# A block of Fourier mixing and latent attention: other queues and engines at the start, queries first, the last rows written directly

## The chip, the cores and the metric

The kernel runs on one core of a Trainium2 chip. The metric is the device time of one execution in microseconds (us); lower is better. The engines are named as in the profile: PE is TensorE's matmul, PEld its weight load, DVE is VectorE, ACT is ScalarE, POOL is GpSimd, and SP is SyncE, which here only issues transfers.

## The reference

One layer of a diffusion backbone: 1024 latent tokens and 256 context tokens, 1024 channels, float32. Cut to what matters:

```python
mod = jax.nn.silu(c) @ w_ada[l] + b_ada[l]
sh_m, sc_m, gt_m, sh_f, sc_f, gt_f = jnp.split(mod[:, None, :], 6, axis=-1)
h_lat = modulate(rms_norm(x, g_pre_mix[l]), sh_m, sc_m)      # h * (1 + scale) + shift
p_lat = h_lat @ w_in[l]
u_f, q_a, kv_a, kr_raw = jnp.split(p_lat, [512, 768, 896], axis=-1)
...
kn_l, v_l = mla_keys_values(kv_a, g_kv_a[l], w_kv_b[l])
qn_l, qr_l = mla_queries(q_a, g_q_a[l], w_q_b[l])            # 8 heads, 64 + 32 channels
attn_l = mla_attention(qn_l, qr_l, k_nope, k_rope, v_all)    # latent and context keys
four_l = fourier_mix(u_f, w_fourier[l])                      # real part of a 2-D DFT, then a map
y_lat = jnp.concatenate([four_l, attn_l], axis=-1) @ w_out[l]
x = x + gt_m * rms_norm(y_lat, g_post_mix[l])
h2 = modulate(rms_norm(x, g_pre_ffn[l]), sh_f, sc_f)
x = x + gt_f * rms_norm(swiglu(h2, w_gate[l], w_up[l], w_down[l]), g_post_ffn[l])
```

## The kernel before, in words

Every matrix product is made of three matmuls: each operand is split into a high part, rounded to PE's fast format, and a low part, the rest (`split`, `mm3`). A letter says which engine makes each part: "a" is ACT, "v" is DVE, "p" is POOL. `mm3` issues high by high (L68), low by high (L69) and high by low (L70).

The scheduler of the language orders the instructions of each engine by the order of the code and their dependences; `pin` keeps some of them in the order of the program. Transfers on SP's queue are issued in their order.

**The sweep (`first_tiles`, 0 to 68 us).** Token tiles 0 and 1 (`xs`, 128x1024 each) are loaded, scaled by their `rstd` and transposed (`xT`). Then eight steps `j`, one for each 128 channels. A step loads a piece of w_ada_mix (`araw`, two transfers of 512 KB) and one of w_in (`wraw`, 128x928), splits both (`ah`, `al`; `win` high and low), multiplies the conditioning vectors by the first (16 matmuls to `aps`), turns the result through `arow` into columns (`cps`), makes shift and scale (`SH`, `A`), modulates (`h`), splits that (`hh`, `hl`) and adds 12 matmuls to `acc`. `modulation` runs two steps ahead of `acc`, the loads three. `constants` loads `rows`, from which the conditioning vectors and biases come.

**The Fourier stage (`fourier`, about 153 to 210 us).** `positions(g)` is the DFT over positions of channel group g (24 matmuls to `po`, `pm`, `pp`; the result `z` is split). `last_turn` transposes the last context tile (`rps`). `attention_weights` loads and splits the weights of queries (`wq`, two pieces `wqraw`), keys (`wk`) and values (`wv`), and the transposed queries, keys and values (`qT`, `kvT`); `kr32T` is the rotary part of the keys, split to `K0h`, `K0l`. Then come `keys([0])` (`kps`, split to `K0h`, `K0l`) and `queries(0)` (`qps`, rotated to `q`, split to `Qh`, `Ql`), and the maps of the Fourier weights (`mps`, split to `map0`, `map1`, from `wfpair` and `ch`). Behind them `channels(g)` (`Sp`, `Co`, `Ce`) is interleaved with the score maxima of head 0 (`greatest`: `sps` on PE, `mx` on DVE).

**The end (`down`).** Eight row tiles i of the output. The last group of products for a half of the columns goes over rows 0 to 7 in the passes n = 2, 5, and for the other half in n = 3, 4. In the last passes each row is added up (V, L1190), its squares are summed on ACT, `rstd` comes from POOL (L1212), DVE multiplies by `rstd` and the gate `Gf` (L1170), and POOL adds the row to `out` by an accumulating DMA (L1171). Only row 7 is multiplied by `Gf` beforehand (L1205, L1209), added to x1, which was loaded back from `out`, and written in two plain halves (L1175, L1176). `finish` handles the row before; it stands ahead of the `rstd` of the present one.

Of the kernel before, what the change touches and what calls it, by code (L numbers as in the profile page):

```python
# [18 lines left out]
P = 128  # L19
D = 1024  # L20
# [19 lines left out]
class Block:  # L40
# [126 lines left out]
    def constants(self):  # L167
        tc, nc, t, cst = self.tc, self.nc, self.t, self.cst
        rows = cst.tile([P, P], F32, name="rows")
        nc.sync.dma_start(rows[0:NROWS, :], t["rows"])  # L170
        self.ident = cst.tile([P, P], F32, name="ident")
        nc.sync.dma_start(self.ident, t["ident"])
        self.comb = cst.tile([4, 2], F32, name="comb")
        self.mhalf = cst.tile([P, 2], F32, name="mhalf")
        nc.vector.memset(self.mhalf, -0.5)
        self.ones = cst.tile([P, P], F32, name="ones")
        nc.vector.memset(self.ones, 1.0)
        nc.scalar.activation(rows[0:16, :], rows[0:16, :], AF.Silu)
# [12 lines left out]
        self.A = cst.tile([P, 2, KT], F32, name="A")  # L191
        self.SH = cst.tile([P, 2, KT], F32, name="SH")
        self.A2 = cst.tile([P, KT], F32, name="A2")
        self.SH2 = cst.tile([P, KT], F32, name="SH2")
        self.Gm = cst.tile([P, D], F32, name="Gm")


    def normed(self, src):
# [3 lines left out]
        nc.sync.dma_start(xs, src)  # L202
# [15 lines left out]
    def first_tiles(self):  # L218
# [8 lines left out]
        def win_split(j):  # L227
# [3 lines left out]
            self.split(wh, wl, raw, "a", "p")  # L231
            return wh, wl
        xT = sw.tile([P, KT, 2 * P], F32, name="xT")
        xs = [self.normed(t["x"][i * P:(i + 1) * P, :]) for i in range(2)]
# [14 lines left out]
        def modulation(j, ah, al):  # L249
# [6 lines left out]
            nc.vector.tensor_copy(row, ps[0:4, 0:256])  # L256
# [7 lines left out]
            nc.vector.tensor_scalar(h, xT[:, j, :], self.A[:, 0, j:j + 1], self.SH[:, 0, j:j + 1], ALU.mult, ALU.add)  # L264
# [210 lines left out]
    def fourier(self):  # L475
# [48 lines left out]
        self.split(wfh, wfl, wf, "a", "p")  # L524
        self.split(chh, chl, ch, "a", "p")
        run(positions(0))
        self.last_turn(bank)
        run(weights)
        run(positions(1))
        run(self.keys([0], bank))  # L530
        run(self.queries(0, bank, self.early, self.early, fp, "raw", "S"))
# [7 lines left out]
        for g in range(4):  # L539
            for work in [channels(g)] + ([positions(g + 2)] if g < 2 else []):  # L540
                for _ in work:

                    steps += 1
                    if steps <= len(KCH) * NT:
                        next(filler)
        run(filler)


    def attention_weights(self):
# [8 lines left out]
        raws = [self.fp.tile([P, D], F32, name="wqraw", tag="X", bufs=2) for _ in range(2)]  # L558
        rawk, rawv = (self.fp.tile([P, 512], F32, name="wkraw", tag="S", bufs=2) for _ in range(2))
        nc.sync.dma_start(rawk, t["w_k"])  # L560
        for k in range(2):
            nc.sync.dma_start(raws[k], t["w_q"][k * P:(k + 1) * P, :])
        nc.sync.dma_start(self.ropeq[64:128, :], t["ropeq"])
        nc.sync.dma_start(rawv, t["w_v"])
        def weight(w, raw, g):

            nc.scalar.activation(w[0], raw, AF.Copy, scale=self.cols[:, g:g + 1])
            nc.vector.scalar_tensor_tensor(w[1], raw, self.cols[:, g:g + 1], w[0].bitcast(F32), ALU.mult, ALU.subtract)
        weight(self.wk, rawk, R_GKV)
        for k in range(2):  # L570
            w = [w[:, k, :] for w in self.wq]
            if k:
                weight(w, raws[k], R_GQ + k)
            else:
                nc.gpsimd.tensor_scalar(raws[k], raws[k], self.cols[:, R_GQ + k:R_GQ + k + 1], 0.0, ALU.mult, ALU.add)
                self.split(*w, raws[k], "a", "p")
            self.split(*(x[:, k, :] for x in self.qT), self.q32[:, k, :], "a", "v")
        yield
        self.split(*self.kvT, self.kv32, "a", "v")
        self.split(kh[64:96, :], kl[64:96, :], self.kr32[64:96, :], "a", "p")  # L580
# [93 lines left out]
    def keys(self, heads, bank):  # L674
        m = 64 * len(heads)
        c = slice(64 * heads[0], 64 * heads[0] + m)
        for c0, n in KCH:
# [3 lines left out]
            for i, h in enumerate(heads):  # L681
                kh, kl = self.K[h % 3]
                self.split(kh[0:64, cs], kl[0:64, cs], ps[i * 64:(i + 1) * 64, 0:n])
# [219 lines left out]
    def all_loads(self):  # L903
# [9 lines left out]
        i = NT - 1  # L913
        yield self.raw(("x1", i), t["out"][i * P:(i + 1) * P, :])
# [195 lines left out]
    def down(self):  # L1110
# [50 lines left out]
        rows = [x[:, q].rearrange("p h c -> p (h c)") for x in (up, low) for q in range(4)]  # L1161
        pending = []

        def finish():

            while pending:
                i, r = pending.pop()
                where = t["out"][i * P:(i + 1) * P, :]
                if i + 1 < NT:
# [4 lines left out]
                for cs in (slice(0, 512), slice(512, D)):  # L1174
# [3 lines left out]
        for n, zh, wh in (2, 0, 0), (5, 1, 1), (3, 0, 1), (4, 1, 0):  # L1178
# [5 lines left out]
            for qs in ([0, 1], [2, 3]) if first else ([0], [1], [2], [3]):  # L1184
# [6 lines left out]
                for q in qs:  # L1191
# [3 lines left out]
                    final = i + 1 == NT  # L1195
                    v = f1.tile([P, 1], F32, name="var", bufs=16)
                    if first:
# [6 lines left out]
                        if final:  # L1204
                            pin(V(c, c, self.Gf[:, cs], ALU.mult))  # L1205
                    else:
                        finish()
                        if final:
                            pin(V(c, c, self.Gf[:, cs], ALU.mult))  # L1209
                        nc.scalar.activation(v, s, AF.Identity, bias=ss[i])  # L1210
                        r = f1.tile([P, 1], F32, name="rstd", bufs=4)
                        pin(nc.gpsimd.tensor_tensor(r, v, self.mhalf[:, 0:1], ALU.pow))  # L1212
                        pending.append((i, r))
# [67 lines left out]
```

## Time and profile before

| what | us |
|---|---|
| median of three runs | 1302.64 (1301.27 to 1303.33) |
| profiled execution, its own time | 1300.21 |
| its span | 1298.4 |
| PE busy | 1222.3 (94%) |
| DVE busy | 934.2 (72%) |
| ACT busy | 633.5 (49%) |
| POOL busy | 479.4 (37%) |
| mean granted clock of PE | 0.982 of full speed |

The span runs from the first instruction to the last event of one profiled execution. Busy times are sums over an engine's instructions; an engine that is not busy waits for another, for a transfer or for its queue. In a timeline a row has the start, the duration, the engine, the line, the operation, and `out<-in` by the program's names; in brackets stands how long the engine had been idle and who ended that.

### The profile page before, as it was taken

Reading aid. Unit: us, or ns where it says so; the run is one execution under the profiler, and the core shown is the slowest. Engines: PE = TensorE matmul, PEld = TensorE weight load, DVE = VectorE, ACT = ScalarE, POOL = GpSimd, SP = SyncE. Lnnn points to the kernel's source line nnn. Section 1 sums busy time; section 2 is a strip of 40 time slices with the busy share of each in tenths; the row PEclk is TensorE's granted clock in tenths of the full one; section 3 lists DMA queues with packets and bytes.
Section 4 is the critical chain, followed back from the end, with each engine's and each line's share of the span. In section 5 each row is a group of like instructions: output and inputs, shape, how many; then the busy total and the mean of one; then the engine's idle time right before and its main releaser. Section 6 shows DMA issues by size and latency. Waiting matters only on the chain.

```text
span 1298.4 us, 15437 instructions
## 1 busy us (share of the span) xinstructions
PE 1222.3 (94%) x5474; PEld 955.1 (74%) x5474; DVE 934.2 (72%) x1301; ACT 633.5 (49%) x1045; POOL 479.4 (37%) x333
## 2 busy tenths in 40 slices
PE   5899978979999999889999999999999999999995
PEld 4588866756666666668788888888888887888884
DVE  6866586687675765353689887777777875898795
ACT  5467747646757668255644444433444433221232
POOL 4365556434555453253263332333311300000173
PEclk9999989989999999999999999999999999999998
DMA  8375211011110104642125554434454468987537
GB/s 318 127 246 169 69 49 36 31 33 46 38 33 17 34 18 139 179 140 101 60 81 179 178 178 149 150 110 144 163 178 154 153 212 335 344 296 256 194 130 130
DMA packets 79369, 181.64 MB, mean 140 GB/s; under 512 B 9569, under 2 KB 41332, under 8 KB 79292
## 3 DMA queue, kind: packets, MB, share of 16 engines
q1 hardware_dynamic: 67228, 137.89, 31.8%
q10 hardware_dynamic: 10800, 39.06, 7.7%
q0 software_dynamic: 1264, 3.70, 1.8%
q8 instruction: 43, 0.70, 0.2%
q14 instruction: 34, 0.28, 0.1%
HBM read 129.15 MB, written 51.48 MB: 139 GB/s over the span
## 4 chain that ended last, share of the span: by engine, by line
PE 49%; issue 2%; ACT 2%; POOL 2%; DVE 1%; DMA 1%; POOLq 0%; DVEq 0%; SPq 0%; ACTq 0%
PE gu L69 10%; PE gu L70 10%; PE gu L68 10%; PE y L774 5%; PE dn L68 4%; PE dn L70 4%; PE dn L69 4%; DMA unit<-zu 1%; DMA raw<-w_down 1%; POOL T L58 0%; POOL out_dram L1171 0%; PE T L209 0%; ACT H L321 0%; POOL rstd L1212 0%; DVE rows L1170 0%
## 5 line engine op out<-in xcount | busy, mean ns | idle before, releaser
L50 ACT ACTIVATE unit<-raw 128x512 fp32r<-128x512 f32 x171 | 105.5, 629 | 226.2 <-PE gu L70 106.3
L58 POOL TENSOR_TENSOR pl<-p,ph 128x1024 fp32r<-128x1024 f32 x53 | 128.8, 2431 | 148.0 <-ACT ph L50 111.6
L56 DVE TENSOR_TENSOR unit<-raw,unit 128x512 fp32r<-128x512 f32 x171 | 149.3, 881 | 27.3 <-ACT unit L50 26.9
L715 DVE TENSOR_REDUCE mx<-sps 128x1 f32<-128x512 f32 (+1 forms) x192 | 105.5, 594 | 31.5 <-PE sps L714 30.6
L640 ACT ACTIVATE p<-S 128x1024 f32<-128x1024 f32 x80 | 81.7, 1022 | 87.1 <-PE S L637 76.6
L935 POOL TENSOR_TENSOR s<-raw 128x512 f32<-128x512 f32 x22 | 33.8, 1537 | 241.4 <-DMA raw<-w_gate 167.9
L1155 POOL TENSOR_TENSOR rows<-rows,acc 128x512 f32<-128x512 f32 x8 | 13.5, 1705 | 212.8 <-DVE acc L1138 211.5
L50 ACT ACTIVATE ph<-p 128x1024 fp32r<-128x1024 f32 x80 | 84.3, 1057 | 1.9
L69 PE MATMUL gu<-T,unit 128*128 128x512 f32 x176 | 69.4, 394 | 0.9 <-POOL T L58 0.9
L70 PE MATMUL gu<-Bh,unit 128*128 128x512 f32 x176 | 69.4, 394 | 0.5 <-DVE unit L56 0.5
L68 PE MATMUL gu<-Bh,unit 128*128 128x512 f32 x176 | 69.4, 394 | 0.0
L69 PE MATMUL gu<-Bl,unit 128*128 128x512 f32 x176 | 69.3, 394 | 0.0
L70 PE MATMUL gu<-T,unit 128*128 128x512 f32 x176 | 69.3, 393 | 0.0
L68 PE MATMUL gu<-T,unit 128*128 128x512 f32 x176 | 69.2, 393 | 0.0
L68 PE MATMUL dn<-unit 128*128 128x512 f32 x148 | 58.2, 393 | 0.4 <-ACT unit L50 0.4
L70 PE MATMUL dn<-unit 128*128 128x512 f32 x148 | 58.0, 392 | 0.0
L69 PE MATMUL dn<-unit 128*128 128x512 f32 x148 | 58.0, 392 | 0.0
L621 PE MATMUL O<-pl,Vh 128*65 128x512 f32 x160 | 53.3, 403 | 4.6 <-POOL pl L58 3.8
L345 PE MATMUL acc<-win,hh 128*128 128x512 f32 (+1 forms) x224 | 55.8, 368 | 0.9 <-ACT hh L50 0.6
L1083 DVE TENSOR_TENSOR u<-u,gu 128x512 f32<-128x512 f32 x66 | 44.8, 681 | 15.6 <-PE gu L70 15.0
L78 POOL TENSOR_TENSOR rstd<-var,mhalf 128x1 f32<-128x1 f32 x44 | 27.6, 629 | 76.3 <-DVE var L76 75.6
L774 PE MATMUL y<-woh,xth 128*128 128x512 f32 x128 | 52.5, 410 | 2.4 <-ACT xth L50 2.4
(425 smaller groups left out, 3552.9 us busy)
## 6 DMA issues: line engine op xcount, KB each, us to landing
zu<-zpair ACTq DMA_DIRECT2D x50, 512.0 KB, 4.3
unit<-zu SPq DMA_DIRECT2D x47, 512.0 KB, 4.6
adraw<-w_ada SPq DMA_DIRECT2D x32, 512.0 KB, 3.9
units<-zu SPq DMA_DIRECT2D x27, 512.0 KB, 5.5
zu<-zone ACTq DMA_DIRECT2D x24, 512.0 KB, 3.1
raw<-w_gate SPq DMA_DIRECT2D x22, 512.0 KB, 4.2
raw<-w_up SPq DMA_DIRECT2D x22, 512.0 KB, 6.3
raw<-w_down SPq DMA_DIRECT2D x22, 512.0 KB, 5.2
```

Source lines behind the costliest of these rows:

```text
L50: nc.scalar.activation(hi, src, AF.Copy)
L56: self.lastv = nc.vector.tensor_tensor(lo, src, hi.bitcast(F32), ALU.subtract)
L58: nc.gpsimd.tensor_tensor(lo, src, hi.bitcast(F32), ALU.subtract)
L68: self.nc.tensor.matmul(out, ah, bh, start=i == 0, stop=False)
L69: self.nc.tensor.matmul(out, ah, bl, start=False, stop=False)
L70: self.nc.tensor.matmul(out, al, bh, start=False, stop=i == n - 1)
L345: nc.tensor.matmul(acc[:, o], a[:, k, :], b[:, k, c], start=k == 0 and n == 0, stop=k == KT - 1 and n == 2)
L621: nc.tensor.matmul(O[0:m, ns], a, b[:, ns], start=k == 0 and i == 0, stop=k == NK - 1 and i == 2)
L640: nc.scalar.activation(p32, S, AF.Exp, scale=SCALE)
L715: nc.vector.tensor_reduce(mx[:, i, c:c + 1], ps[:, 0:n], AX.X, ALU.max)
L774: nc.tensor.matmul(ps[:, ns], u[:, k, :], w[:, k, ns], start=k == 0 and i == 0, stop=k == KT - 1 and i == 2)
L1083: V(d, d, ps, ALU.add)
```

## The change

Three places are changed.

In the sweep `rows` is loaded with 96 partitions (padded by zeros) instead of 83; the two `xs` are loaded on ACT's queue; the low part of `win` is made by DVE instead of POOL; `arow` and `h` are made by ACT instead of DVE.

In the Fourier stage the queries of head 0 come right behind `last_turn`, then the keys of head 0, then positions(1). The keys' low parts are put off to step 4 of the interleaved part, the values' weight and the low part of the rotary key behind the second `yield`, to step 8. `wqraw` is in tiles of its own and loaded ahead of `w_k`; both pieces go through `weight` (ACT scales, DVE subtracts). The low parts of `wfpair` and `ch` are made by DVE.

At the end rows 4 to 7 are finished as row 7 was: x1 is loaded, DVE multiplies by `Gf` into the free tiles `a[6]` and `a[1]`, and one product (two halves for row 7) adds x1 and is written without accumulation. `finish` comes behind `rstd`.

```diff
@@ constants, normed, first_tiles
-        nc.sync.dma_start(rows[0:NROWS, :], t["rows"])
+        nc.sync.dma_start(rows[0:96, :], t["rows"])
...
-        nc.sync.dma_start(xs, src)
+        (queue or nc.sync).dma_start(xs, src)
...
-            self.split(wh, wl, raw, "a", "p")
+            self.split(wh, wl, raw, "a", "v")
...
-        xs = [self.normed(t["x"][i * P:(i + 1) * P, :]) for i in range(2)]
+        xs = [self.normed(t["x"][i * P:(i + 1) * P, :], nc.scalar) for i in range(2)]
...
-            nc.vector.tensor_copy(row, ps[0:4, 0:256])
+            nc.scalar.activation(row, ps[0:4, 0:256], AF.Copy)
...
-            nc.vector.tensor_scalar(h, xT[:, j, :], self.A[:, 0, j:j + 1], self.SH[:, 0, j:j + 1], ALU.mult, ALU.add)
+            nc.scalar.activation(h, xT[:, j, :], AF.Identity, bias=self.SH[:, 0, j:j + 1], scale=self.A[:, 0, j:j + 1])
@@ fourier
-        self.split(wfh, wfl, wf, "a", "p")
-        self.split(chh, chl, ch, "a", "p")
         run(positions(0))
         self.last_turn(bank)
-        run(weights)
+        run(self.queries(0, bank, self.early, self.early, fp, "raw", "S"))
+        next(weights)
+        lows = []
+        run(self.keys([0], bank, lows))
         run(positions(1))
-        run(self.keys([0], bank))
-        run(self.queries(0, bank, self.early, self.early, fp, "raw", "S"))
+        self.split(wfh, wfl, wf, "a", "v")
+        self.split(chh, chl, ch, "a", "v")
...
+                    if steps == 4:
+                        for low in lows:
+                            low()
+                    elif steps == 8:
+                        run(weights)
@@ attention_weights
-        raws = [self.fp.tile([P, D], F32, name="wqraw", tag="X", bufs=2) for _ in range(2)]
+        raws = [e.tile([P, D], F32, name="wqraw", tag=tag, bufs=1) for tag in ("Ql0", "raw")]
-        nc.sync.dma_start(rawk, t["w_k"])
         for k in range(2):
             nc.sync.dma_start(raws[k], t["w_q"][k * P:(k + 1) * P, :])
+        nc.sync.dma_start(rawk, t["w_k"])
...
+        for k in range(2):
+            self.split(*(x[:, k, :] for x in self.qT), self.q32[:, k, :], "a", "v")
+        for k in range(2):
+            weight([w[:, k, :] for w in self.wq], raws[k], R_GQ + k)
         weight(self.wk, rawk, R_GKV)
-        for k in range(2):
-            w = [w[:, k, :] for w in self.wq]
-            if k:
-                weight(w, raws[k], R_GQ + k)
-            else:
-                nc.gpsimd.tensor_scalar(raws[k], raws[k], self.cols[:, R_GQ + k:R_GQ + k + 1], 0.0, ALU.mult, ALU.add)
-                self.split(*w, raws[k], "a", "p")
-            self.split(*(x[:, k, :] for x in self.qT), self.q32[:, k, :], "a", "v")
         yield
         self.split(*self.kvT, self.kv32, "a", "v")
-        self.split(kh[64:96, :], kl[64:96, :], self.kr32[64:96, :], "a", "p")
+        nc.scalar.activation(kh[64:96, :], self.kr32[64:96, :], AF.Copy)
+        yield
+        nc.vector.tensor_tensor(kl[64:96, :], self.kr32[64:96, :], kh[64:96, :].bitcast(F32), ALU.subtract)
         weight(self.wv, rawv, R_GKV)
@@ all_loads
-        i = NT - 1
-        yield self.raw(("x1", i), t["out"][i * P:(i + 1) * P, :])
+        for i in range(NT // 2, NT):
+            yield self.raw(("x1", i), t["out"][i * P:(i + 1) * P, :])
@@ down
-        rows = [x[:, q].rearrange("p h c -> p (h c)") for x in (up, low) for q in range(4)]
+        rows = [up[:, q].rearrange("p h c -> p (h c)") for q in range(4)]
+        rows += [a[n][:, q:q + 2].rearrange("p q c -> p (q c)") for n in (6, 1) for q in (0, 2)]
...
-                if i + 1 < NT:
+                if i < NT // 2:
...
-                for cs in (slice(0, 512), slice(512, D)):
+                for cs in [slice(0, 512), slice(512, D)] if i + 1 == NT else [slice(0, D)]:
...
+                    if zh:
+                        pin(V(rows[i][:, cs], c, self.Gf[:, cs], ALU.mult))
...
-                        finish()
-                        if final:
-                            pin(V(c, c, self.Gf[:, cs], ALU.mult))
                         nc.scalar.activation(v, s, AF.Identity, bias=ss[i])
                         r = f1.tile([P, 1], F32, name="rstd", bufs=4)
                         pin(nc.gpsimd.tensor_tensor(r, v, self.mhalf[:, 0:1], ALU.pow))
+                        finish()
                         pending.append((i, r))
```

One step of the sweep on DVE, before:

```order
L256 COPY arow<-aps 4x256
L56 TENSOR_TENSOR al<-araw,ah 128x1024
L261 TENSOR_SCALAR SH<-cps,cols 128x2
L262 TENSOR_SCALAR A<-cps,b_86,cols 128x2
L56 TENSOR_TENSOR al<-araw,ah 128x1024
L264 TENSOR_SCALAR h<-xT,A,SH 128x256
L56 TENSOR_TENSOR hl<-h,hh 128x256
```

The same engine in a step of the changed kernel:

```order
L56 TENSOR_TENSOR win_103<-wraw,win_102 128x928
L56 TENSOR_TENSOR al<-araw,ah 128x1024 x2
L56 TENSOR_TENSOR hl<-h,hh 128x256
L261 TENSOR_SCALAR SH<-cps,cols 128x2
L262 TENSOR_SCALAR A<-cps,b_86,cols 128x2
```

`arow` and `h` have left DVE, and the subtraction of `win` has come to it.

In the Fourier stage ACT's order, before, from the weight of the keys on:

```order
L567 ACTIVATE wkh<-wkraw,cols 128x512
L50 ACTIVATE zh<-pp 128x2x130
L382 ACTIVATE kv32T<-rps 128x128
L383 ACTIVATE kr32T<-rps 32x128
L50 ACTIVATE kvTh<-kv32T 128x1280
L50 ACTIVATE K0h<-kr32T 32x1280
L50 ACTIVATE wqh<-wqraw 128x1024
L567 ACTIVATE wqh<-wqraw,cols 128x1024
L567 ACTIVATE wvh<-wkraw,cols 128x512
```

In the changed kernel, from the same copies of the last transposition on:

```order
L382 ACTIVATE kv32T<-rps 128x128
L383 ACTIVATE kr32T<-rps 32x128
L50 ACTIVATE kvTh<-kv32T 128x1280
L575 ACTIVATE wqh<-wqraw,cols 128x1024 x2
L575 ACTIVATE wkh<-wkraw,cols 128x512
L584 ACTIVATE K0h<-kr32T 32x1280
L575 ACTIVATE wvh<-wkraw,cols 128x512
```

Both `wqh` now stand directly behind `kvTh`. On PE the 12 `qps` follow the last `rps`, then 9 `kps`, then the 24 matmuls of positions(1); before, it was positions(1), `kps`, `qps`.

At the end POOL's order, before, in its last part:

```order
L1212 TENSOR_TENSOR rstd<-var,mhalf 128x1
L1171 DMA out_dram<-rows_9079 128x1024
L1212 TENSOR_TENSOR rstd<-var,mhalf 128x1
L1171 DMA out_dram<-rows_9079 128x1024
L1212 TENSOR_TENSOR rstd<-var,mhalf 128x1
```

In the changed kernel, from the third last DMA on:

```order
L1186 DMA out_dram<-rows_9077 128x1024
L1223 TENSOR_TENSOR rstd<-var,mhalf 128x1
L1186 DMA out_dram<-rows_9077 128x1024
L1223 TENSOR_TENSOR rstd<-var,mhalf 128x1
L1186 DMA out_dram<-rows_9077 128x1024
L1223 TENSOR_TENSOR rstd<-var,mhalf 128x1 x3
```

Four accumulating DMAs are left of seven, each behind the `rstd` of the row after its own, and the last three `rstd` follow each other.

## Rows read from the trace of the kernel before

**Rows 1.** The page's busy time, share of the span and instructions of each engine.

```profile
PE 1222.3 (94%) x5474; PEld 955.1 (74%) x5474; DVE 934.2 (72%) x1301; ACT 633.5 (49%) x1045; POOL 479.4 (37%) x333
```

**Rows 2.** Waits of PE over the span: total us, times, longest.

```profile
PE aps L254 <- DVE al L56: 5.5, 6, 1.6
...
PE Sp L70 <- DVE map1l L56: 2.2, 1, 2.2
```

**Rows 3.** Timeline of DVE, then POOL, in the sweep: start us, duration us.

```profile
25.18 1.21 DVE L56 TENSOR_TENSOR al<-araw,ah 128x1024 fp32r<-128x1024 f32 x1
...
30.54 2.73 DVE L56 TENSOR_TENSOR al<-araw,ah 128x1024 fp32r<-128x1024 f32 x1
...
30.01 2.19 POOL L58 TENSOR_TENSOR win<-wraw,win 128x928 fp32r<-128x928 f32 x1 [5.03 <-ACT win L50]
...
56.68 2.19 POOL L58 TENSOR_TENSOR win<-wraw,win 128x928 fp32r<-128x928 f32 x1 [4.70 <-ACT win L50]
```

**Rows 4.** Groups from 0 to 62 us: busy, mean ns, idle before.

```profile
L58 POOL TENSOR_TENSOR win<-wraw,win 128x928 fp32r<-128x928 f32 x8 | 19.2, 2399 | 28.5 <-ACT win L50 28.5
...
L50 ACT ACTIVATE hh<-h 128x256 fp32r<-128x256 f32 x7 | 2.9, 417 | 24.0 <-DVE h L264 24.0
```

**Rows 5.** Busy us of PE, PEld, DVE, ACT, POOL by stretch; clock, DMA share, GB/s.

```profile
26.40:68.30 41.90, 36.56 (x207) 26.30 (x207) 30.65 (x45) 21.42 (x33) 14.72 (x9) 0.96 0.42 145
28.14:61.10 32.96, 28.06 (x165) 19.82 (x165) 27.50 (x36) 15.32 (x20) 11.20 (x5) 0.98 0.47 168
157.40:180.00 22.60, 15.00 (x66) 10.99 (x65) 17.87 (x24) 14.94 (x26) 10.98 (x6) 0.92 0.21 64
169.10:173.10 4.00, 4.00 (x11) 3.15 (x12) 3.98 (x8) 0.59 (x1) 2.33 (x2) 0.57 0.00 0
179.60:198.60 19.00, 19.00 (x101) 16.39 (x99) 15.43 (x31) 6.93 (x18) 11.35 (x17) 0.91 0.22 84
```

**Rows 6.** Timeline of PE, then ACT, ahead of the first head.

```profile
157.52 0.27 PE L379 MATMUL rps<-ident,R 128*32 128x128 f32 x1
...
169.10 0.50 PE L70 MATMUL qps<-qTh,wql 128*128 128x512 f32 x1 [4.29 <-POOL wql L58]
...
158.64 0.73 ACT L567 ACTIVATE wkh<-wkraw,cols 128x512 fp32r<-128x512 f32 x1
...
160.12 1.28 ACT L50 ACTIVATE kvTh<-kv32T 128x1280 fp32r<-128x1280 f32 x1
...
162.72 1.06 ACT L50 ACTIVATE wqh<-wqraw 128x1024 fp32r<-128x1024 f32 x1
```

**Rows 7.** Timeline of PE, POOL and DVE at the end.

```profile
1283.66 0.39 PE L69 MATMUL dn<-units,unit 128*128 128x512 f32 x1
1283.88 0.39 PE L70 MATMUL dn<-units,unit 128*128 128x512 f32 x1
...
1286.58 0.89 POOL L1171 DMA_DIRECT2D out_dram<-rows  x1 [1.62 <-DVE rows L1170]
...
1289.67 0.89 POOL L1171 DMA_DIRECT2D out_dram<-rows  x1 [1.62 <-DVE rows L1170]
...
1286.20 0.68 DVE L1190 TENSOR_TENSOR rows<-rows,dn 128x512 f32<-128x512 f32 x1
1288.09 1.28 DVE L1170 SCALAR_TENSOR_TENSOR rows<-rows,rstd,Gf 128x1024 f32<-128x1024 f32 x1 [1.22 <-POOL rstd L1212]
...
1291.18 1.42 DVE L1175 SCALAR_TENSOR_TENSOR raw<-rows,rstd,raw 128x512 f32<-128x512 f32 x2 [1.21 <-POOL rstd L1212]
```

**Rows 8.** Timeline of ACT and SP at the start, PE at the sweep's end.

```profile
9.52 1.06 ACT L50 ACTIVATE ah<-araw 128x1024 fp32r<-128x1024 f32 x1 [0.80 <-DMA araw<-w_ada_mix]
10.80 1.06 ACT L50 ACTIVATE ah<-araw 128x1024 fp32r<-128x1024 f32 x1 [0.23 <-DMA araw<-w_ada_mix]
...
1.61 0.89 SPq L202 DMA_DIRECT2D xs<-x  x2
...
67.71 0.58 PE L290 MATMUL acc<-win,hl 128*128 128x512 f32 x2
```

More of the change, by code (lines that the diff above doesn't have):

```diff
@@ L195, in constants, with normed @@
         self.Gm = cst.tile([P, D], F32, name="Gm")
-    def normed(self, src):
+    def normed(self, src, queue=None):
         nc = self.nc
         xs = self.xp.tile([P, D], F32, name="xs", bufs=2)
-        nc.sync.dma_start(xs, src)
+        (queue or nc.sync).dma_start(xs, src)
         r = self.rstd(self.xp, self.meansq(self.xp, xs, D))
@@ L672, in prepare, with keys @@
         yield from self.greatest(h, self.bankW, self.ap)
-    def keys(self, heads, bank):
+    def keys(self, heads, bank, lows=None):
         m = 64 * len(heads)
@@ L682, in keys @@
                 kh, kl = self.K[h % 3]
-                self.split(kh[0:64, cs], kl[0:64, cs], ps[i * 64:(i + 1) * 64, 0:n])
+                src = ps[i * 64:(i + 1) * 64, 0:n]
+                self.nc.scalar.activation(kh[0:64, cs], src, AF.Copy)
+                low = lambda kh=kh, kl=kl, cs=cs, src=src: self.nc.vector.tensor_tensor(kl[0:64, cs], src, kh[0:64, cs].bitcast(F32), ALU.subtract)
+                if lows is None:
+                    low()
+                else:
+                    lows.append(low)
             yield
@@ L1194, in down @@
                     s = self.meansq(f1, c, D, 512)
-                    final = i + 1 == NT
+                    if zh:
+                        pin(V(rows[i][:, cs], c, self.Gf[:, cs], ALU.mult))
                     v = f1.tile([P, 1], F32, name="var", bufs=16)
@@ L1203, in down @@
                                 pin(add(x, x, a[7][:, q, :], ALU.add))
-                        if final:
-                            pin(V(c, c, self.Gf[:, cs], ALU.mult))
-                    else:
-                        finish()
-                        if final:
-                            pin(V(c, c, self.Gf[:, cs], ALU.mult))
+                    else:
                         nc.scalar.activation(v, s, AF.Identity, bias=ss[i])
@@ L1259 @@
     }
-    arrays["rows"] = np.concatenate([a[k].reshape(-1, P) for k in ("c", "c_ctx", "g_pre_mix", "g_pre_ffn", "b_ada", "g_q_a", "g_kv_a")])
+    rows = np.concatenate([a[k].reshape(-1, P) for k in ("c", "c_ctx", "g_pre_mix", "g_pre_ffn", "b_ada", "g_q_a", "g_kv_a")])
+    arrays["rows"] = np.concatenate([rows, np.zeros((96 - NROWS, P), rows.dtype)])
     arrays["w_ada_mix"] = arrays["w_ada"][:, :2 * D].reshape(KT, P, 2, KT, P).transpose(3, 1, 0, 2, 4)
```

## The prediction

> **What bounds the kernel now.** The page comes first: it shows that PE is at work for 94% of the span [rows 1]. So time can be had only where PE stands still, and the change touches three such places: the sweep (the first 68 us), the stretch ahead of the first head in the Fourier stage (157 to 180 us), and the last rows (from the last matmul to the end). The middle keeps its order on every engine, so it only shifts.
>
> In the sweep I looked next at PE's waits. The largest entry of this part is for `al`, the low half of a piece of w_ada_mix, which DVE makes [rows 2]. The timeline says why DVE is late. The same 128x1024 subtraction takes 1.21 us alone and 2.73 us when it starts 0.53 us after POOL's `win` subtraction [rows 3]; it ends at 33.27, and POOL's ends at 32.20, so about 1.07 us after POOL is done. The two don't share, DVE stands still while POOL works. The eight POOL subtractions are 2.4 us each [rows 4], one per step, and a step takes (56.68 − 30.01) / 4 = 6.67 us [rows 3]. In five steps DVE is busy 27.50 of 32.96 us, PE 28.06, ACT 15.32 [rows 5]: DVE, blocked part of the time, and PE, which waits for it in turn, set the step together; ACT has room.
>
> In the Fourier stage the same kind of wait stands alone: PE starts the queries, then waits 4.29 us for POOL's `wql` [rows 6]. The windows show the cost twice: 15.00 of 22.60 us busy from 157.4 to 180, and after the wait a clock of 0.57 from 169.1 to 173.1, half of the 2.4 GHz level for most of these 4 us [rows 5].
>
> At the end PE is done at 1283.88 + 0.39 = 1284.27, and the span goes on to 1298.4. The accumulating DMAs on POOL start 3.09 us apart, while a row of PE needs 12 matmuls spaced 0.22 us, 2.7 us [rows 7]. So a queue has grown by the time PE ends: the last two products end at 1291.18 + 1.42 = 1292.60, 8.33 us after PE, and 5.8 us of DMA follow.
>
> **The change part by part: the sweep.** It moves `win`'s low part from POOL to DVE, and `arow` and `h` from DVE to ACT; the x tiles go to ACT's queue, so that SP issues the first `araw` first.
>
> The start: before, transfers of 512 KB land 1.28 us apart (ACT begins `ah` as they land, 9.52 and 10.80), and the two x tiles are ahead of them [rows 8]. With two queues I let each x tile land with one `araw`: first `araw` at 7.6, second at about 10.1. From there DVE's order decides, by rows: `ah` 1.06 and `al` 1.2 bring the second `al` to 12.3; behind it stand up to the last `al` of step 2 two copies of the same size, two `win` (1.1 each, by 928 of 1024 columns of the 1.21), four `al`, and small ones of about 0.4 twice, some 10 us. That `al` ends at about 22.3; before, it was 25.18 + 1.21 = 26.4 [rows 3].
>
> From 26.4 to 68.3, where the last matmul of the first two tiles ends [rows 8], PE is busy 36.56 us and idle 5.34, at a mean clock of 0.96 [rows 5]. ACT and DVE must not be in its way: per step ACT has 15.32 / 5 = 3.1 us and gets `h` and `arow`, each priced as `hh`, 0.42 [rows 4], so 3.9; DVE has two `al`, `win` and the small ones, 2.4 + 1.1 + 0.9 = 4.4 us unblocked; PE needs 28.06 / 5 = 5.6 with the tails of single matmuls in it. So PE would bound the step. I leave it 1 us of waits for `arow`, whose way now goes through ACT behind 1.06 us copies, and take 0.6 us for a clock that doesn't dip. End at 22.3 + 36.6 + 0.4 = 59.3: **9 us less**. Bounds: 12.5 if also the tails fall away (a step of 5.0), 5 if the step stays at 6.
>
> The Trainium skill, page "Trainium Kernel Development and Optimization", section Key Constraints, speaks against the move of queues: transfers from several queues share the same 16 engines, and issuing from several saves only issue time. By that rule the two tiles give back the 0.89 us of their issue [rows 8] and no landing, and the sum would be some 1 us smaller. No row here has two queues at the start.
>
> **The Fourier stage.** Five POOL operations go to DVE or fall away; positions(1), 24 matmuls that hid ACT and DVE after the last `rps`, now comes behind the queries and keys. What is late next is the weight's high part. PE ends `rps` at 157.52 + 0.27 = 157.8. ACT still makes `kvTh` first, at 160.12 less the 0.7 of `wkh` that no longer stands ahead, so until 160.7, then `wqh` 1.06: first query at about 161.8 [rows 6]. That is **a new wait of 4 us** at the place where there was none. DVE then needs `kvTl` and two weights of 1.28 each, as the same shape has at the end [rows 7], until about 164.8, which holds up the 12 query matmuls by 1.1 more. The keys need nothing that is late, and behind them positions(1) hides DVE's rotary products and `Qh`; the maps then wait some 2.2 as now [rows 2]. PE's work is 15.0 less 1.7 (the 4.0 us at 0.57 would be 2.3 at full clock): 13.3. So 157.4 + 13.3 + 4.0 + 1.1 + 2.2 = 178.0 against 180.0. **2 us less.** Whether the clock falls again after the new wait is open: a stretch like the present one costs 1.7. The three low parts of the keys and the values' weight, put behind, cost DVE about 2.4 us, under 19.0 − 15.43 = 3.6 us of its idle time from 179.6 to 198.6 [rows 5]; without that cover they would lengthen the stage by as much. Bounds: 4 less, 2 more.
>
> **The end.** Rows 4 to 7 are finished without accumulation: DVE multiplies by `Gf` while the sum of squares is under way, and one product adds x1 and goes out by a plain DMA. POOL does `rstd` for the next row ahead of the DMA, so nothing in its order holds back a row. Six more 128x512 products at 0.68 on DVE [rows 7] fit: per row 0.6 + 0.6 + 1.2 = 2.4 us as they follow each other, under the 2.7 of PE. Above that they would add to the end row by row. After PE's end the last row needs V 0.7, ACT's sum 1.1, `rstd` 0.9 and its products 1.4, 4.2 us in all; the price of ACT's sum is a bound from what lies now between V's start at 1286.20 and the product at 1291.18, 4.98 us, in which also the POOL DMA (0.89) and its wait for the product (1.62) stand [rows 7]: 4.98 − 2.5 + 1.4 gives 3.9. With 4.2 instead of 8.33: **4.1 us less**, bounds 3 and 5. Three more loads of x1, 1.5 MB, come on SP some 100 us before; a wait of 4 us would show if they held a weight.
>
> **Sum.** 9 + 2 + 4.1 = 15.1 us off the profiled 1300.21, 1285.1. The median of the runs shown is 2.4 above the profiled one, so 1287.5.
>
> **Rivals.**
> *The sweep keeps a step of 6 us.* `h` and `arow` now stand in ACT's order between copies that wait for DMA; if a loop `arow`, `cps`, `SH`, `A`, `h` sets the step, PE keeps half its waits. For: PE's waits at present are all on such small handoffs. Against: ACT is only 46% busy in these steps [rows 5]. Gain 5 instead of 9: 1291.5. Chance 0.2.
> *The new wait eats the Fourier stage.* If the weights come 2 us later and the clock falls for 4 us a second time, the 2 us gain becomes 2 lost: 1291.5. Against: `wqh` waits for one copy only. Chance 0.13.
> *The end does not do what it says.* If the accumulating DMA of row 3 or the plain writes, now closer together, land later than 5.8 us, the 4.1 go: 1291.6. For: the DMAs of the last rows already lie behind each other. Against: the plain rows have half the traffic of an accumulation. Chance 0.08.
> *Slower.* DVE becomes the bound of the sweep: it takes eight `win` and is blocked no more, but if its subtraction of 928 columns took the 2.4 us that POOL takes and `al` stayed at its contended 2.7, a step would be 2.4 + 5.4 + 0.9 = 8.7 us, 2 us above the present; it decides from 6.67 + 15.1 / 8 = 8.6 on. 1304. Against: POOL has no SBUF subtraction left in these steps. Chance 0.04.
>
> **How the numbers follow.** The forecast has the other 0.55, with 1284 to 1291 as its own range. The range of 1282 to 1294 takes in the better bounds (12.5 + 2 + 4.5 is 19, 1283.6; one more for the spread of runs) and two of the rivals together in part. About 0.2%, 2.6 us, is what a measurement of this kernel can tell from no change: faster by more 0.94, within 0.02, slower 0.04.
>
> **What would show it.** In the changed profile: no DVE subtraction above 1.3 us before 60; the last matmul of the first tiles near 59; a PE wait of about 4 us for ACT's `wqh` near 149 (shifted by the 9), with a stretch of low clock behind it or not; DVE's last product 4.2 us after PE's last matmul. I am wrong if the sweep ends after 63, if the wait ahead of the queries is above 6 us, or if the last product comes over 6 us after PE.

## The result, and the profile after

The changed kernel takes 1281.8 us (median of 4 runs, 1280.09 to 1283.03); the kernel before took 1301.95 in the runs beside them. The ratio is 0.9845 [0.9827, 0.9864]: 20.15 us faster, where 15.1 were forecast, and 0.2 us under the range. The median lies 5.7 us under the forecast's 1287.5: 5.05 of them are gain, and 0.7 is the kernel before, which took 1302.64 in the runs that the forecast counted from. The changed kernel's profiled execution took 1283.03 us, with a span of 1281.3 and a mean clock of 0.981.

The page's busy times answer to [rows 1]:

```profile
PE 1222.5 (95%) x5474; PEld 957.9 (75%) x5474; DVE 926.2 (72%) x1303; ACT 639.9 (50%) x1061; POOL 452.5 (35%) x317
```

PE has as much work as before, so what was gained is idle time. Four marks on PE divide the span into five parts, each mark read in both traces (us from the start of the span):

| from the start to | before | after | gained | of it in this part |
|---|---|---|---|---|
| end of the first tiles' last matmul (`acc`) | 68.29 | 58.38 | 9.9 | 9.9 |
| start of the last `rps` | 157.52 | 150.51 | 7.0 | −2.9 |
| first `tps` (the first head's first transposition of scores) | 200.93 | 189.37 | 11.6 | 4.5 |
| end of the last matmul | 1284.27 | 1273.26 | 11.0 | −0.55 |
| end of the span | 1298.4 | 1281.3 | 17.1 | 6.1 |

So the profiled pair shows 17.1 of the 20.15. The fourth part, 1084 us long, keeps PE's order and still differs by 0.55; how far it varies by itself stands in the last section.

PE's waits over the whole span answer to [rows 2] (total us, times, longest); shown are the largest, which is in the middle (10.8 us before), and those of the changed places that the text comes back to:

```profile
PE sps L727 <- DVE mx L728: 11.9, 7, 6.6
...
PE aps L253 <- ACT ah L50: 3.4, 1, 3.4
PE xT L209 <- ACT h L321: 3.4, 1, 3.4
...
PE qps L68 <- ACT wqh L575: 3.0, 1, 3.0
...
PE Sp L68 <- ACT map1h L50: 1.0, 1, 1.0
```

The waits for `al` (5.5 us), for `wql` (4.3) and for `map1l` (2.2) are gone. The wait for `h` behind the sweep was 1.1 and has grown to 3.4; the one for `wqh` is new; the one for `ah` is the first step's, at 9.10.

Stretches of the changed kernel (length, busy us of PE, PEld, DVE, ACT, POOL, then clock, DMA share, GB/s), to be held against [rows 5]:

```profile
20.00:40.00 20.00, 19.51 (x129) 14.75 (x130) 18.24 (x27) 16.85 (x27) 0.00 (x0) 1.00 0.99 345
58.00:70.00 12.00, 8.63 (x32) 7.42 (x31) 7.34 (x22) 11.89 (x36) 7.80 (x12) 0.72 0.61 222
61.74:68.00 6.26, 6.25 (x21) 5.62 (x22) 5.76 (x18) 6.16 (x21) 4.42 (x7) 0.52 0.45 154
167.90:189.37 21.47, 19.17 (x109) 16.62 (x110) 19.18 (x42) 7.84 (x20) 14.17 (x22) 1.00 0.20 74
1272.00:1276.00 4.00, 1.26 (x6) 0.72 (x4) 3.77 (x4) 1.40 (x5) 1.77 (x2) 1.00 0.94 321
```

In the middle of the sweep PE is at work for 19.51 of 20 us; DVE is busy for 18.24 there, and the DMA engines are full (0.99). Right behind the sweep there is a hole: from 61.74 to 68 the granted clock is 0.52, which is the 1.2 GHz level for nearly all of it. In the Fourier stage the stretch from the first `Sp` on is at full clock.

### The profile page after: what moved, and what is told of

It reads as the page before. It is cut to its first block, busy times and chain, and to the rows that moved or that the text cites. A ratio compares the mean times of both kernels' runs of the same rounds, so it can differ in the third digit from the quotient of the medians.

```text
span 1281.3 us, 15462 instructions
## 1 busy us (share of the span) xinstructions
PE 1222.5 (95%) x5474; PEld 957.9 (75%) x5474; DVE 926.2 (72%) x1303; ACT 639.9 (50%) x1061; POOL 452.5 (35%) x317
## 4 chain that ended last, share of the span: by engine, by line
PE 53%; ACT 1%; issue 1%; DMA 1%; DVE 1%; POOL 1%; POOLq 0%; DVEq 0%; ACTq 0%
PE gu L69 10%; PE gu L70 10%; PE gu L68 10%; PE y L787 6%; PE dn L68 5%; PE dn L69 5%; PE dn L70 5%; DMA unit<-zu 1%; POOL T L58 0%; PE T L209 0%; ACT H L321 0%; ACT unit L50 0%; ACT T L50 0%; ACT T7h L50 0%; PE gps L449 0%
```

## The experiments

Each was run beside the kernel before on the same chip; ratios are to that kernel, and the times of two runs are compared by them, since `e9` to `e11` ran on another chip than the rest. Labels name the runs.

**The three parts, each alone.** The kernel before with only the edits of the first 68 us (`e1_sweep`), only those of the Fourier stage (`e2_fourier`), only those of the end (`e3_end`); the edits are the hunks of the diff above.

> Only the changes of the first 68 us. Theory: the sweep itself is 9.9 us shorter, as in the changed kernel's trace, and about 2.9 us of it are handed back right behind it, where ACT waits for the x tile of a later step ahead of the modulation and PE then runs at half clock; so 7 us less, about 1295 (ratio 0.9945). Rival: what is handed back belongs to another part of the change, then 9 to 10 us less, about 1292.

> Only the Fourier stage's changes. Theory from the changed kernel's trace: 3.0 us up to the first Ce product and 1.5 more up to the transposition of the maxima, so 4.5 us less, about 1297.5 (ratio 0.9965), with a PE wait of 3 us for wqh. Rival, as forecast: 2 us less or, with a second stretch at half clock, nothing.

> Only the last rows' changes. Theory from the changed kernel's trace: 5.4 us less, about 1296.5 (ratio 0.996): 3.1 us because the last product follows PE's end by 5.2 us instead of 8.3, and 2.3 because the last DMA lands 3.5 us behind it instead of 5.8. Rival, as forecast: the landing stays at 5.8, then 3 to 4 us less.

| run | median us | ratio | gained |
|---|---|---|---|
| e1_sweep | 1293.01 | 0.9938 [0.9921, 0.9955] | 0.62%, 8.1 us |
| e2_fourier | 1295.87 | 0.9957 [0.9943, 0.9971] | 0.43%, 5.6 us |
| e3_end | 1295.38 | 0.9951 [0.9932, 0.9970] | 0.49%, 6.4 us |

The parts add up to 1.54%, and the whole gives 1.55%. The intervals of the three together leave about 0.3%, 4 us, and within that the parts don't act on one another. Against the forecast only the Fourier stage is clear of the noise by its time: 5.6 us, by its interval 3.8 to 7.4, for the 2 that were forecast. The intervals of the sweep (5.9 to 10.3) and of the end (3.9 to 8.8) hold the forecast's 9 and 4.1; what those parts did is read from traces below. In e3's trace the last product comes 4.49 us after PE's end, not the 5.2 of its expectation.

**The sweep without one of its edits.** `e11_sweep_win_pool` is e1 with `win`'s low part left to POOL, `e10_sweep_one_queue` is e1 with the x tiles left on SP's queue:

```diff
@@ e11_sweep_win_pool, against e1_sweep
-            self.split(wh, wl, raw, "a", "v")
+            self.split(wh, wl, raw, "a", "p")
@@ e10_sweep_one_queue, against e1_sweep
-        xs = [self.normed(t["x"][i * P:(i + 1) * P, :], nc.scalar) for i in range(2)]
+        xs = [self.normed(t["x"][i * P:(i + 1) * P, :]) for i in range(2)]
```

> The sweep's changes, but the low part of win is made by POOL again; arow and h stay on ACT. Theory: POOL's subtraction holds DVE's al for up to 2 us per step as before, so the step stays near 6 us and the sweep's end near 64, 5 us of the 9 are lost. Rival: with arow and h off DVE the blocked DVE is hidden, and the sweep ends near 59 as in the changed kernel.

> The sweep's changes without the move of the x tiles to ACT's queue (they are issued first by SP again). Theory: the queue gave only its issue time and the earlier first transfer of araw, under 1.5 us at the end of the sweep: sweep's end near 60, 7 us less than before. Rival, as in the forecast's working of the start: the queue is worth 2 us or more at the sweep's end.

With POOL's `win` the kernel took 1298.05, 0.9981 [0.9969, 0.9993]: of 0.62% some 0.19% is left. POOL's `win` comes every 5.5 us (35.07, 40.60, 46.11, 51.64), and the sweep ends at 61.56 instead of 58.90. So both theories were half right: the other edits alone take the step from 6.67 to 5.5, but the last `rps` starts at 155.11 instead of 149.66, and most of the part's gain hangs on `win`. In these steps it is no longer `al` that stands still beside POOL's `win`, but the small `hl`, which took 0.42 us at 34.08 before:

```profile
35.33 2.23 DVE L56 TENSOR_TENSOR hl<-h,hh 128x256 fp32r<-128x256 f32 x1 [0.72 <-ACT hh L50]
```

With the x tiles back on SP's queue it took 1287.27, 0.9896 [0.9872, 0.9919]: 0.42% better than e1, which neither the theory nor the rival had. The sweep ends at 56.91 instead of 58.90, and the last `rps` starts at 146.14 instead of 149.66.

**The hole behind the sweep.** In the changed kernel's trace ACT shows what PE waits for (start, duration, and in brackets the idle time before):

```profile
57.15 1.06 ACT L86 ACTIVATE junk<-xs 128x1024 bf16<-128x1024 f32 x1 [4.19 <-DMA xs<-x]
58.11 0.19 ACT L86 ACTIVATION_READ_ACCUMULATOR junk<-xs 128x1 f32 x1
58.21 1.83 ACT L321 ACTIVATE h<-xT,SH,A 128x128 f32<-128x128 f32 x5
```

`junk` is the sum of squares of a later x tile. Its load is issued late, as it waits for a free buffer: SP's row of three such loads lasts 19.63 us, where the issue of one takes 0.33 elsewhere.

```profile
34.10 19.63 SPq L202 DMA_DIRECT2D xs<-x  x3
```

So the tile lands late; ACT stands 4.19 us in its order, and the modulation `h` of tile 2 stands behind it. `e4_hold` keeps these ACT instructions in the order of the program, so that the later tile's sum of squares comes behind `h`; `hold` is on only up to the first step of the loop over the later tiles and the sum of squares issued there:

```diff
@@ meansq
-        self.nc.scalar.activation(junk, src, AF.Square, scale=float(n) ** -0.5, accum_out=ss)
+        a = self.nc.scalar.activation(junk, src, AF.Square, scale=float(n) ** -0.5, accum_out=ss)
+        if getattr(self, "hold", False):
+            self.tc.keep_in_program_order(a)
@@ the loop over the later tiles
+        self.hold = True
...
+            self.hold = False
@@ modulate
-            self.nc.scalar.activation(out, ps[:, k * P:(k + 1) * P], AF.Identity, bias=shift[:, k:k + 1], scale=scale[:, k:k + 1])
+            a = self.nc.scalar.activation(out, ps[:, k * P:(k + 1) * P], AF.Identity, bias=shift[:, k:k + 1], scale=scale[:, k:k + 1])
+            if getattr(self, "hold", False):
+                self.tc.keep_in_program_order(a)
```

> The changed kernel, with the sum of squares of the x tile after next held behind the modulation of tile 2 on ACT. Theory: the PE wait of 3.4 us for ACT's h behind the sweep falls to about 1 us and the half clock behind it goes, so 2 to 4 us less than the changed kernel, about 1279 (ratio 0.982). Rival: the following tile then waits for its x as long, and nothing is won, about 1282.

In the trace `h` starts at 53.61 and PE's wait is gone. PE begins the next tile's transpositions (`xT`) at 70.88 instead of 76.34, 5.5 us earlier. Up to the last `rps`, at 147.11 instead of 150.51, 2.1 us of that are lost again, 1.5 of them from 131.62 on, where the clock fell once more:

```profile
140.00:143.00 3.00, 3.00 (x15) 2.94 (x15) 0.00 (x0) 0.43 (x3) 0.88 (x2) 0.51 0.69 193
```

In time it is 1281.01, 0.9838 [0.9821, 0.9856], within the interval of the changed kernel. The later stretch from the first `tps` to PE's end, whose order the edit doesn't touch, took 1085.48 in this trace against 1083.89, which used up half of the 3.4 us that were left. So the cause of the hole is shown; its worth in time is not, by this run alone.

**The weight ahead of the queries.** `e5_wq_pool` is the changed kernel with `wqh` made by POOL, so that it doesn't stand behind `kvTh` on ACT; `e6_both` has e4's and e5's edits together:

```diff
-            nc.scalar.activation(w[0], raw, AF.Copy, scale=self.cols[:, g:g + 1])
+            if g < R_GKV:
+                nc.gpsimd.tensor_scalar(w[0], raw, self.cols[:, g:g + 1], 0.0, ALU.mult, ALU.add)
+            else:
+                nc.scalar.activation(w[0], raw, AF.Copy, scale=self.cols[:, g:g + 1])
```

> The changed kernel, with the high parts of both query weights made by POOL, which is idle there, instead of ACT behind kvTh. Theory: the 3.0 us wait of PE ahead of the queries falls under 1 us, the stretch at half clock behind it (about 6 us long) goes, and 4 us or more are won up to the first head, so about 1278. Rival: the low parts on DVE are the next thing late, the wait only moves to the matmuls with wql, and 1 us or less is won.

> The held sum of squares (e4) and the query weights on POOL (e5) together. Theory: both waits and both half-clock stretches go, so 3 us from the one and 4 from the other, about 1275 (ratio to before 0.979). Rival: the waits behind take them up, no better than the single edits, about 1280.

e5: 1282.96, 0.9870 [0.9852, 0.9888], no gain. PE's waits in its trace say why:

```profile
PE qps L70 <- DVE wql L579: 1.8, 2, 1.2
...
PE Sp L68 <- ACT map1h L50: 1.7, 1, 1.7
...
PE qps L68 <- POOL wqh L576: 1.1, 1, 1.1
```

The 3.0 us for `wqh` and 1.0 for `map1h` became 1.1 for `wqh`, 1.8 for `wql` and 1.7 for `map1h`: the wait went to what is late next, as the rival had it. e6 took 1277.77, 0.9823 [0.9806, 0.9839], between its theory and its rival and the lowest of the three, but its interval still meets e4's; that the moved weight pays once the hole is closed isn't settled, and e13 below speaks against it.

**The changed kernel once more.** `e7_again`, without an edit, gives a second trace.

> The changed kernel once more, unedited, for a second trace of it beside e4, e5 and e6. Theory: stretches of half clock in the middle, where the order is that of the kernel before, differ from trace to trace by 1 to 2 us in sum without an edit there, so this trace has the waits of the first one and another sum of half-clock time. Rival: the same stretches as in the first trace, within 0.5 us.

1281.99, 0.9861 [0.9845, 0.9876]. Its marks are 61.21, 151.98, 190.28 and 1271.86 with the clock at 0.987: the sweep ended 2.8 us later than in the first trace, and the 1084 us of the middle were 2.3 us shorter. A mark of a single trace is no surer than that.

**The order of the Fourier stage.** `e8_positions_first` is the changed kernel with positions(1) ahead of the queries again; `e14_no_put_off` is e2 with the keys' low parts and the values' weight made at once:

```diff
@@ e8_positions_first, against the changed kernel
+        run(positions(1))
         run(self.queries(0, bank, self.early, self.early, fp, "raw", "S"))
...
-        run(positions(1))
@@ e14_no_put_off, against e2_fourier
-        run(self.keys([0], bank, lows))
+        run(self.keys([0], bank))
+        run(weights)
...
-                    if steps == 4:
-                        for low in lows:
-                            low()
-                    elif steps == 8:
-                        run(weights)
```

> The changed kernel, but positions(1) ahead of the queries as before; engines, loads and put-off low parts stay. Theory: the gain of the Fourier stage came from the rotary products and the maps, which positions(1) hides when it comes behind the queries; here PE waits again some 3 us ahead of the maps' products and the wait for wqh is gone, so about 2 us are given back, 1284. Rival: the gain came from the engines alone, then as the changed kernel or faster, since the wait for wqh is hidden.

> The Fourier stage's changes alone, as e2, but the keys' low parts and the values' weight made at once and not put off. Theory: the order (positions(1) behind the queries) made the gain, and DVE has 3 us more ahead of the maps, of which positions(1) hides most: 1 us or less worse than e2, about 1297. Rival: the putting off made half of the gain, 1298.5.

e8: 1285.03, 0.9876 [0.9862, 0.9891]; from `rps` to `tps` 41.11 us, against 38.86 and 38.30 in the two traces of the changed kernel. Its wait for `wqh` is only 0.4, but waits for `kvTl` and `map1l` of 1.2 each are back. By these marks the order is worth the 2 us of the theory. But the intervals of the times meet (e7's ends at 0.9876, where e8's median lies), and e8's stretch has a fall of the clock of its own, to 0.77 and 0.80 from 166 to 174, so the size is no surer than that.

e14: 1302.91, 1.0020 [1.0011, 1.0029]. With the stage's other edits in place, putting things off is worth all its 5.6 us and more, against both expectations. What the edits of engines and loads bring by themselves, or the putting off without them, wasn't run. The trace of e14 shows PE's longest wait in this stage, then DVE and POOL at that place:

```profile
PE mps L69 <- DVE wfpair L56: 3.9, 1, 3.9
```

```profile
173.97 0.75 DVE L572 SCALAR_TENSOR_TENSOR wvl<-wkraw,cols,wvh 128x512 fp32r<-128x512 f32 x1
...
175.90 2.20 DVE L56 TENSOR_TENSOR wfpair<-wfraw,wfpair 128x512 fp32r<-128x512 f32 x1
...
175.21 2.34 POOL L58 TENSOR_TENSOR Ql<-q,Qh 96x1024 fp32r<-96x1024 f32 x1 [17.35 <-ACT Qh L50]
```

DVE makes `wvl`, needed much later, ahead of the maps' `wfpair`; so `wfpair` comes beside POOL's `Ql` and takes 2.20 us, where the like `zl` of 128x512 takes 0.68 in the same trace (at 174.64), and ends 0.55 us after POOL's. That is the standstill of [rows 3] again. The Trainium skill, page "SBUF — State Buffer", section "Who interferes with whom", calls the port pair that the two engines share an exclusive lock; 2.73 us before and 2.20 here agree with it.

**The end, split.** `e9_finish_only` is the kernel before with `finish()` behind the next row's `rstd`, and nothing else; `e15_direct_only` is e3 with `finish()` ahead of it:

```diff
@@ e9_finish_only, against the kernel before
-                        finish()
                         if final:
...
                         pin(nc.gpsimd.tensor_tensor(r, v, self.mhalf[:, 0:1], ALU.pow))
+                        finish()
```

> The kernel before, with only finish moved behind the rstd of the present row; all rows but the last still go out by accumulating DMAs. Theory: POOL then keeps pace with PE's 2.7 us a row (DMA 0.9 and rstd 0.55 to 0.9 with no wait between), so the last product follows PE's end by about 5 us as in the changed kernel, but the landing of the last DMAs stays near 5.8 us: 3 us less, about 1298. Rival: the gain is all in the plain writes, then no change.

> The end's changes alone, as e3, but finish ahead of the present row's rstd as before. Theory: rows 4 to 7 go out by plain writes at twice the rate of the accumulating ones, so the landing is 3.5 us behind the last product; but that product comes later than the 4.5 us of e3, since rstd waits for nothing but stands behind the product of the row before on no engine but POOL, where only four DMAs are left: 1 us or less worse than e3, about 1296. Rival: without the earlier rstd the end is that of the kernel before plus 2.3, about 1299.

| | last product's end after PE's end | from there to the span's end | together | ratio |
|---|---|---|---|---|
| before | 8.33 | 5.80 | 14.13 | |
| e9_finish_only | 4.79 | 7.95 | 12.74 | 0.9990 [0.9980, 1.0000] |
| e15_direct_only | 6.78 | 3.52 | 10.30 | 0.9963 [0.9950, 0.9976] |
| e3_end | 4.49 | 3.48 | 7.97 | 0.9951 [0.9932, 0.9970] |
| changed kernel | 4.50 | 3.54 | 8.04 | |

The order of `finish` brings the last product forward, by 3.5 us with accumulating writes (8.33 to 4.79) and by 2.3 with plain ones (6.78 to 4.49); the plain writes alone do so by 1.6 (8.33 to 6.78). Without plain writes most of it is lost again: the DMA engines stay full, and the end of the span comes 7.95 us behind the last product instead of 5.80. In time e9 gained 0.1%, with an interval that reaches no change, where its theory had 3 us; e15 came out as its theory had it, within the noise. The windows of the kernel before and of e9, both from 1288 to 1292, have the DMA engines full at half the rate of the changed kernel:

```profile
1288.00:1292.00 4.00, 0.00 (x0) 0.00 (x0) 2.70 (x4) 0.02 (x1) 1.53 (x3) 0.64 1.11 177
```

```profile
1288.00:1292.00 4.00, 0.00 (x0) 0.00 (x0) 1.65 (x3) 0.00 (x0) 0.89 (x1) 0.68 0.99 167
```

That is 177 and 167 GB/s at a share of about 1, against 321 at 0.94 in the changed kernel, whose last accumulating write is issued at 1268.12, so that plain ones make up most of that window.

**A better kernel.** `e12_one_queue` is the changed kernel with the x tiles on SP's queue (e10's edit), `e13_one_queue_wq` has e5's edit as well.

> The changed kernel with the x tiles issued by SP again, ahead of the first araw. Theory: as in e10 the sweep ends near 57 and, since the sum of squares of the later x tile then stands behind the modulation in ACT's order, no wait of PE for ACT's h follows; 4 to 5 us less than the changed kernel, about 1277. Rival: the sweep's gain in e10 is taken up by the Fourier stage, whose weights land at the same time, 1281.

> e12 with the query weights' high parts on POOL as in e5. Theory: as e12 within 1.5 us, since e5 showed that the wait only moves to the low parts. Rival: without the first half-clock stretch the second one goes too, 2 us better than e12.

e12: 1276.83 (1274.77 to 1277.92), 0.9817 [0.9803, 0.9831], the lowest median of all. It lies below both medians of the changed kernel by 5 us, by ratio 3.6 and 5.7; its interval and that of the first comparison overlap slightly, that of e7 lies clear of it. e13 is the same, 1277.39, 0.9832 [0.9812, 0.9852]. In e12's trace, behind the sweep, the window of PE and then ACT:

```profile
58.00:70.00 12.00, 12.00 (x67) 10.69 (x66) 9.51 (x22) 9.76 (x28) 9.75 (x12) 1.00 0.81 277
```

```profile
54.16 1.85 ACT L321 ACTIVATE h<-xT,SH,A 128x128 f32<-128x128 f32 x5 [0.60 <-PE xT L209]
...
59.44 1.11 ACT L86 ACTIVATE junk<-xs 128x1024 bf16<-128x1024 f32 x1
```

The late `junk` now stands behind `h`, and PE works 12.00 of 12 us at full clock. The changed kernel worked for 8.63 us in that window, 6.25 of them at 0.52: counted at full clock 2.38 + 6.25 × 0.52 = 5.6 us of work against 12.0. The difference, 6.4 us, is nearly all of the 6.6 by which the last `rps` starts earlier (143.91 against 150.51).

## Why the prediction was right and where it failed

**The sweep** ran as its steps had it. DVE makes `al` and `win` without standing still:

```profile
25.09 2.35 DVE L56 TENSOR_TENSOR al<-araw,ah 128x1024 fp32r<-128x1024 f32 x2
28.02 1.11 DVE L56 TENSOR_TENSOR win<-wraw,win 128x928 fp32r<-128x928 f32 x1
```

That is 1.2 us for each `al`, 1.11 for `win`. `ah` started at 7.99 and 9.99 (forecast 7.6 and 10.1), the second `al` of step 2 ended at 23.83 (22.3), and PE's last matmul of these tiles at 58.38 (59.3). That this last number came so close is in part luck. The start was 1.5 us late by a wait that the sum doesn't have: DVE copies the second tile's `xT` only when PE has transposed it.

```profile
15.34 1.23 DVE L239 COPY xT<-xT 128x1024 f32<-128x1024 f32 x1 [1.91 <-PE xT L209]
```

From 23.83 on PE needed 34.55 us, where the sum had 37.0, since a step became shorter than its 5.6: `win` comes every 5.09 us.

```profile
32.52 1.12 DVE L56 TENSOR_TENSOR win<-wraw,win 128x928 fp32r<-128x928 f32 x1
...
47.78 1.12 DVE L56 TENSOR_TENSOR win<-wraw,win 128x928 fp32r<-128x928 f32 x1
```

This step refutes two of the rivals, a step kept at 6 us and a DVE that becomes the bound at 8.6.

What failed here was taking the end of the sweep for the end of the matter: "The middle keeps its order on every engine, so it only shifts." Between the sweep's end and the last `rps` 2.9 us were handed back (1.5 in e7's and e1's traces), in the wait for `h` and the low clock after it. And the step "With two queues I let each x tile land with one `araw`" had the first `ah` about right and missed the cost: e10 and e12 show that the move of queues loses some 4 to 6 us, in both contexts. The Trainium skill, page "Trainium Kernel Development and Optimization", section Key Constraints, has issue from several queues save only issue time. The runs go further than that: the two loads' issue was saved, and the program became slower. What the move did to the instructions is shown, the place of `junk` ahead of `h` on ACT. e4 takes back that one thing and starts the next tile's `xT` 5.5 us earlier than the changed kernel, at 70.88; e12 starts it at 69.77, 1.1 us earlier still, as its sweep ends 1.1 us before e4's (57.49 against 58.61). With two queues the second x tile's `junk` stands behind the first `ah` (8.95 us, in e12 at 7.36), and the first `win` begins at 16.48 instead of 15.24. Why the scheduler chose these orders isn't shown.

**The Fourier stage** is the step that failed by most. It was "the maps then wait some 2.2 as now", and the putting off, which was costed at neither gain nor loss. The 1.1 us for `wql` didn't come either: the changed kernel's trace has no such wait, e7's one of 0.5. PE's timeline:

```profile
150.51 0.27 PE L379 MATMUL rps<-ident,R 128*32 128x128 f32 x1
...
153.83 0.80 PE L68 MATMUL qps<-qTh,wqh 128*128 128x512 f32 x1 [3.05 <-ACT wqh L575]
...
167.90 0.50 PE L68 MATMUL Sp<-zh,map1h 128*128 128x512 f32 x1 [0.99 <-ACT map1h L50]
...
189.37 0.27 PE L733 MATMUL tps<-ident,m 128*8 128x128 f32 x1 [2.30 <-DVE m L731]
```

The new wait came, 3.05 us instead of 4. The clock fell again behind it, as the open point feared: the first such `qps` takes 0.80 us, and from 150.78 to 167.90 the mean clock was 0.80 (before, 0.90 over the like 17.5 us). So up to `Sp` little was gained, 17.39 against 17.77 us from the start of `rps`. The gain lies behind: from `Sp` to `tps` 21.47 instead of 25.64 us, 4.2 of the stage's 4.5. The wait of 2.19 us for `map1l` is gone, and so is the low clock that followed it (a mean clock of 0.93, now 1.00). The window of before for that stretch:

```profile
175.29:200.93 25.64, 21.16 (x108) 17.74 (x109) 20.35 (x43) 9.07 (x20) 14.53 (x22) 0.93 0.17 62
```

The low clock, some 1.6 us of these 4.2, doesn't always come. e10, e11 and e15 have the stage's old order and a wait of 2.1 us for `map1l` as well, but kept the full clock behind it and took 41.8 us from `rps` to `tps`; the kernel before, e1, e3 and e9 took 43.4 to 43.9. The traces with the new stage took 38.1 to 39.0, so 3 to 5 us less.

The reason lies on DVE. In the kernel before, `wvl` stood ahead of the maps and beside POOL's `wql`:

```profile
166.77 2.83 DVE L568 SCALAR_TENSOR_TENSOR wvl<-wkraw,cols,wvh 128x512 fp32r<-128x512 f32 x1
...
165.84 3.20 POOL L58 TENSOR_TENSOR wql<-wqraw,wqh 128x1024 fp32r<-128x1024 f32 x1
```

DVE had hardly a gap from there to `map1l`, at 177.46. With the three low parts of the keys (1.60) that is 4.4 us of DVE ahead of it, which the forecast counted as 2.4 and only at their new place, where `wvl` takes 0.74. e14, which puts them back, has the maps late again. The rule that work put behind costs nothing if it is covered was used on the place it went to; the place it came from had PE waiting.

**The end.** The last product came 4.50 us after PE, forecast 4.2:

```profile
1272.87 0.39 PE L70 MATMUL dn<-units,unit 128*128 128x512 f32 x1
...
1276.35 1.41 DVE L1190 SCALAR_TENSOR_TENSOR raw<-acc,rstd,raw 128x512 f32<-128x512 f32 x2 [0.44 <-POOL rstd L1223]
```

The failed step is "and 5.8 us of DMA follow": it became 3.54. The rival had looked for a later landing and was wrong for the full change; e9 shows that it is what happens with accumulating writes, 7.95. So this term was 6.1 instead of 4.1: 3.8 by the product and 2.3 by the landing, which the sum had at nothing.

**The sum.** By each part's own run: sweep 8.1 for 9, Fourier 5.6 for 2, end 6.4 for 4.1, together 20.1 for 15.1. By its interval each of the three can be off by about 2 us, so the Fourier stage and the landing at the end are the terms that the record shows as mis-sized, and the sweep's 8.1 is no sure miss. The better end of the range was 12.5 + 2 + 4.5: it let the sweep grow, which it didn't, and held the Fourier stage at its 2, where 4 was its own better bound and 5.6 came.

## What to carry to other kernels

Work put off is a gain of its own wherever its old place delays something a bottleneck engine waits for: cost both places. When several accumulating writes end a kernel, look at the rate in the window after the last product: if the DMA share is full and the rate low, plain writes shorten the landing as well. After moving a load to another queue, read the order of the in-order engines behind that stage again, since an instruction that waits for a late transfer can have moved ahead of one that is ready.

## What the runs showed of the hardware beyond this

A DMA share of about 1 doesn't mean one rate: 177 GB/s with accumulating writes into the output (1288 to 1292 before), 321 with mostly plain ones (1272 to 1276 in the changed kernel), 345 in the sweep's loads.

The time of an unchanged order varies by traces. From the first `tps` to PE's end it was 1083.34 us before, and 1083.89, 1081.58, 1084.88, 1082.26, 1083.65 and 1085.48 in the changed kernel, e7, e1, e2, e3 and e4, which have the same order there. The clock isn't shown to be the reason: the mean granted clock of this stretch reads 0.99 in all of them, which is too coarse to tell, and by the mean over the span e14, with 0.978, has 1081.98 us, and e8, with 0.987, has 1085.40. What decides in a given execution whether the clock falls after a wait stays open.
